# One attention layer of an encoder trunk: TensorE's order in the attention stage written by streams with an account of time, weighing on ScalarE, modulations' totals behind their sums

## The chip, the cores and the metric

The kernel runs on one core of one Trainium2 chip. The core has five engines that run side by side: TensorE (PE, matrix products; PEld is its loading of weights), VectorE (DVE), ScalarE (ACT), GpSimd (POOL) and SyncE (SP), which here issues the DMAs. Each engine works off its own queue in order, and waits at an instruction whose inputs or whose place for the output are not ready. The metric is the time of one execution in microseconds (us).

## What is computed

A trunk of two layers over 256 tokens of 1024 channels: an RWKV-7 layer and an attention layer, each followed by a mixture of experts with 32 experts of 256 hidden channels. The change lies in the attention layer, whose mixer is this:

```python
def dilated_attention_mix(h, w_qkv, w_o):
    qkv = jnp.einsum('bsd,de->bse', h, w_qkv)
    qkv = qkv.reshape(bsz, s, N_GROUPS, 3, ATTN_HEADS, ATTN_HEAD_DIM)      # 3 groups, 8 heads of 128
    for gi, (window, dil) in enumerate(((128, 1), (512, 4), (2048, 16))):
        o, lse = _dilated_group(q, k, v, slopes[gi], window, dil)            # softmax over a window, with ALiBi
    alpha = jax.nn.softmax(jnp.stack(lses), axis=0)                          # groups merged per head
    merged = jnp.sum(alpha[..., None] * o, axis=0).reshape(bsz, s, d)
    return jnp.einsum('bsd,de->bse', merged, w_o)
```

Every sub-layer is normalised, and modulated by six vectors that are products of `silu(c)` with matrices of 1024 x 1024:

```python
    mod = silu_c @ ada_w[i] + ada_b[i]
    sh_t, sc_t, ga_t, sh_c, sc_c, ga_c = jnp.split(mod, 6, axis=-1)
    x = x + ga_t * tm
```

Four of the attention layer's six, numbers m = 2 (`ga_t`), 3, 4 and 5, are computed during its attention, since nothing needs them earlier: `ga_t` is needed by the output weights, 3 and 4 by the router of the experts behind, 5 by those experts.

## The kernel before

The program is four stages in a row: RWKV, its experts (moe 0), attention, its experts (moe 1). The text below is on the attention stage, which in the trace runs from about 675 to 951 us.

**Products in halves.** All attention products are made of two fp16 halves of each operand: `triple` (L1712) issues three matmuls, high x high and the two mixed ones. So every tensor has to be split: `split` (L461) writes the high half on ScalarE (`wh`, `qh`, `eh`, `mh`) and the low half on VectorE (`wl`, `ql`, `el`, `ml`), or, for one half of some weights, on GpSimd.

**Projections.** `project(hp, g)` makes for a pair of heads hp (of four) and a group g (of three) the queries, keys and values, j = 0, 1, 2: 36 projections b = 9 hp + 3 g + j. Each takes one weight tile of 1 MB (`wring`), which is split in two halves; the split halves have three places (`WB`). Each is 48 matmuls of 256 columns into one PSUM bank; there are three such banks (`pp`), and a bank is free again when its projection has been split into `qh`, `ql`. The four output products of the stage's end use the same three banks and one more.

**Scores and merge.** `scores` makes the scores of a (hp, g), 12 matmuls, adds the ALiBi bias (`E`, VectorE, L1800), takes the row maximum (`st`) and the exponential with its sums (ScalarE, L1809). When all three groups of a pair are there, `merge` computes the groups' weights (`mm`, `wg`, `den`: a chain of small VectorE instructions, with one on ScalarE in it). `values(hp, a)`, for each head a of the pair, multiplies the exponentials by these weights, twelve instructions per pair on VectorE (L1837), transposes them on TensorE (`eT`), splits them (`eh`, `el`), multiplies by the values (`av`, 18 matmuls) and splits the result (`mh`, `ml`). The output product (`wo`) uses `mh`, `ml` and the output weights, which GpSimd first multiplies by the gate `ga_t` (`gated`, L583).

**Modulations.** A modulation is 8 tiles of 512 KB (`aring`). `ada` (L428) adds each, times `silu`, to an accumulator `acc` on VectorE, in two half sums of 512 columns (L374 for the first tile, L376 for the others: 64 in the stage). With the eighth tile the total over the partitions is made at once by TensorE (`ada` in the trace: 2 matmuls of 512 columns, or 8 of one column), and VectorE adds the bias. There is one accumulator, so the next modulation's first sum waits until the total has been read.

**What sets the order.** A scheduler places the instructions on the engines; it works with priorities from the order in which the program is written, and with costs of its own. In this stage nothing is pinned: the loop over hp and g below writes projections, then scores of the group before, then four modulation tiles (`ADA_PARTS`); merge and values come at the end of a pair. In the RWKV stage another way is used: `weave` runs several generators (streams), keeps an account of TensorE's time from estimates per matmul, and at each step continues the stream of best rank (`RANK`) that is due. A generator yields either a number, the time in us after which it wants to go on, or a condition. During `weave` TensorE's instructions keep the order in which they are written (`on_pe`); for the other engines the account sets priorities, moved by `OFFSET`.

**DMA.** SyncE issues all weight loads, each waiting until its buffer is free. The weight stream runs through all stages, so the first tiles of moe 1 are loaded while the last projections run; further buffers are added as areas of the attention stage come free (`middle`, `ext`).

Of the kernel before, what the change touches and what calls it, by code (L numbers as in the profile page):

```python
# [10 lines left out]
F32 = mybir.dt.float32  # L11
I32 = mybir.dt.int32
F16 = mybir.dt.float16
# [6 lines left out]
D = 1024  # L20
# [214 lines left out]
def trunk(ctx, tc, names, aps, out, stages=("rwkv", "moe0", "attn", "moe1"), dbg=None, ring=2):  # L235
# [192 lines left out]
    def ada(i, m, k, tag="ps"):  # L428
# [9 lines left out]
        if k < KD - 1:  # L438
            return
        if m in (2, 5):  # L440
            g = gates[i, m] = const.tile([128, D], F32, name=f"ga{m}", tag=f"ga{m}", bufs=1)
            bias = nc.scalar.dma_start(out=g, in_=ap["p_adab"][i:i + 1, m * D:(m + 1) * D].to_broadcast([128, D]))
            tc.keep_in_program_order(bias)
            for c in range(2):
                s = slice(c * 512, c * 512 + 512)
                ps = bank(name="ada", tag=tag)
                mm(ps, ONES, acc[:, s])
                V.tensor_tensor(out=g[:, s], in0=g[:, s], in1=ps, op=ALU.add)
        else:
# [1272 lines left out]
    def heads(outer, mh, ml, before, c4):  # L1722
# [45 lines left out]
        def project(hp, g):  # L1768
            out = []
            for j in range(3):  # L1770
                with tc.issue_after(heads.hi[5].ins) if hp + g == 0 and j == 1 else nullcontext():
                    w = heads.w if hp + g + j == 0 else weights(
                        outer, stream.take(("qkv", hp, g, j)).rearrange("p (k n) -> p k n", k=KD),
                        pool_half=j != 1 and hp + g > 0)
                ps = bank(name="qkv", tag="pp")
                t = [(held, pool)[j // 2].tile([128, 2, S], F16, name=f"q{n}{g}{j}", bufs=1) for n in "hl"]
                for k in range(KD):
                    hk = (hh[:, k], hl[:, k])
                    lhs, rhs = (w[k], hk) if j < 2 else (hk, w[k])
# [4 lines left out]
                split(*(v.rearrange("p a n -> p (a n)") for v in t), ps, (scale if j == 0 else 1.0) / WSC)  # L1784
                out.append(t)
            return out

        def scores(hp, g, qkv, E, st):

            q, k, _ = qkv  # L1790
            w = KW[g]
            for a in range(2):
# [10 lines left out]
                V.tensor_reduce(out=st[:, :, a, 0], in_=e, axis=AX.X, op=ALU.max)  # L1803
            neg = pool.tile([128, NTT, 2], F32, name="neg", bufs=2)
# [26 lines left out]
        def values(hp, a, qkv, E, wg):  # L1831

            eh, el = (pool.tile([128, 8, 128], F16, name=n) for n in ("eh", "el"))
            for g in range(3):
                for t in range(NTT):
                    e = E[g][:, a, t * KW[g]:(t + 1) * KW[g]]
                    V.tensor_scalar(out=e, in0=e, scalar1=wg[:, t, g, a:a + 1], scalar2=None, op0=ALU.mult)  # L1837
            blocks = [E[0][:, a, t * 256 + kt * 128:t * 256 + kt * 128 + 128] for kt in range(2) for t in range(NTT)]
            blocks += [E[g][:, a, t * 128:(t + 1) * 128] for g in (1, 2) for t in range(NTT)]
            for n in range(2):  # L1840
# [3 lines left out]
                split(*(v[:, 4 * n:4 * n + 4].rearrange("p b n -> p (b n)") for v in (eh, el)), ps, WSC)  # L1844
            po = bank(name="av", tag="eT")
            vcol = slice(a * 128, a * 128 + 128)

            def av(o, v, c, start, stop):
                triple(o, [t[:, v[1], vcol] for t in qkv[v[0]][2]],
# [4 lines left out]
            for g in (1, 2):  # L1854
                for t in range(NTT):
# [3 lines left out]
                  po[:, 0:S].rearrange("p (r l) -> p r l", r=NTT), 1.0 / WSC)  # L1859

# [4 lines left out]
        attn_shares = iter(ADA_ATTN)  # L1865
        for hp in range(4):
            if hp == 3:
                modulations_attn[0].done()
                apool1.release()
                if "moe1" in stages:  # L1870
                    ext.extend(middle(1, 0))
            qkv, E, st = [], [], []
            for g in range(4):
                if g < 3:
                    qkv.append(project(hp, g))
                for n in range(max(0, g - 1), g):
                    E.append(pool.tile([128, 2, NTT * KW[n]], F32, name=f"E{n}", bufs=1))
                    st.append(pool.tile([128, NTT, 2, 2], F32, name=f"st{n}", bufs=2))
                    scores(hp, n, qkv[n], E[n], st[n])
                if g < 3 and hp < 3:  # L1880
                    for a in itertools.islice(attn_shares, ADA_PARTS[3 * hp + g]):
                        ada(*a, "ada")
            if hp == 3:
                held.release()
                if "moe1" in stages:
                    ext.extend(middle(1, 4))
            wg = merge(st)
            for a in range(2):
                values(hp, a, qkv, E, wg)
            if hp == 3:  # L1890
                po = {(t, c): bank(name="wo", tag="ada" if t + c == 2 else "pp")
                      for t in range(NTT) for c in range(2)}
                for _ in out_pairs(outer, range(3), po, mh, ml):
                    pass
# [204 lines left out]
```

## Time and profile before

| | us |
|---|---|
| three runs | 1184.41, 1186.47, 1190.94 (median 1186.47) |
| the profiled execution | 1182.29, of which its span 1180.5 |
| attention stage in the span | about 675 to 951 |
| experts behind it (moe 1) | about 964 to 1180 |

| engine | busy us of the span | share |
|---|---|---|
| PE | 1040.8 | 88% |
| DVE | 616.8 | 52% |
| ACT | 432.4 | 37% |
| POOL | 148.7 | 13% |

The span is the time from the first to the last instruction; the 1.8 us by which the execution is longer lie around it. Busy shares are averages over stages with different limits, so each stage has to be read for itself. Matmuls are pipelined, and their shown durations overlap: a projection's matmul is shown with some 273 ns, and the next starts 109 ns later. Where a line is that of a helper (L271 is every matmul), the group is told by its tiles' names.

### The profile page before, as it was taken

Reading aid. Unit: us, or ns where it says so; the run is one execution under the profiler, and the core shown is the slowest. Engines: PE = TensorE matmul, PEld = TensorE weight load, DVE = VectorE, ACT = ScalarE, POOL = GpSimd, SP = SyncE. Lnnn points to the kernel's source line nnn. Section 1 sums busy time; section 2 is a strip of 40 time slices with the busy share of each in tenths; the row PEclk is TensorE's granted clock in tenths of the full one; section 3 lists DMA queues with packets and bytes.
Section 4 is the critical chain, followed back from the end, with each engine's and each line's share of the span. In section 5 each row is a group of like instructions: output and inputs, shape, how many; then the busy total and the mean of one; then the engine's idle time right before and its main releaser. Section 6 shows DMA issues by size and latency. Waiting matters only on the chain.

```text
span 1180.5 us, 25023 instructions
## 1 busy us (share of the span) xinstructions
PE 1040.8 (88%) x10580; PEld 682.5 (58%) x10580; DVE 616.8 (52%) x1458; ACT 432.4 (37%) x915; POOL 148.7 (13%) x110
## 2 busy tenths in 40 slices
PE   7789999998978998978987799899979999789886
PEld 2576677766757655435442388777858754354422
DVE  4864678578485446213111467988885762131112
ACT  2634455455445342101000377555544621010012
POOL 1100010010012600000000112123373000000000
PEclk9879899899988899989999999998989999899999
DMA  9561524325233676998999987877744589989995
GB/s 366 207 220 60 180 67 159 114 89 167 73 130 132 263 286 250 400 414 361 422 421 421 420 346 262 310 268 284 255 173 150 212 352 395 416 362 421 420 421 238
DMA packets 53197, 322.01 MB, mean 273 GB/s; under 512 B 5922, under 2 KB 6562, under 8 KB 21458
## 3 DMA queue, kind: packets, MB, share of 16 engines
q1 hardware_dynamic: 51986, 315.88, 68.7%
q0 software_dynamic: 800, 3.36, 0.8%
q8 instruction: 87, 1.43, 0.5%
q10 hardware_dynamic: 288, 1.05, 0.3%
q14 instruction: 36, 0.29, 0.1%
HBM read 319.22 MB, written 1.05 MB: 271 GB/s over the span
## 4 chain that ended last, share of the span: by engine, by line
PE 23%; DMA 21%; DVE 8%; ACT 2%; issue 1%; ACTq 0%; SPq 0%; DVEq 0%
DMA wring<-in_w_moe_dram 21%; PE qkv L271 11%; PE gu L271 3%; DVE acc L376 2%; PE xT L271 1%; PE wo L271 1%; DVE wl L473 1%; PE acc L271 1%; PE dn L271 1%; PE av L271 1%; PE eT L275 1%; PE sc L271 1%; ACT sq L491 0%; DVE ql L473 0%; DVE E L1837 0%
## 5 line engine op out<-in xcount | busy, mean ns | idle before, releaser
L271 PE MATMUL gu<-wring,xT 128*32 128x512 f32 x1024 | 132.5, 617 | 18.0 <-DMA wring<-in_w_moe_dram 10.8
L376 DVE SCALAR_TENSOR_TENSOR acc<-aring,silu,acc 128x512 f32<-128x512 f32 x140 | 116.1, 859 | 13.2 <-DMA aring<-in_w_ada_dram 13.0
L467 POOL TENSOR_TENSOR wl<-wring,wh 128x1024 f16<-128x1024 f32 x24 | 57.7, 2406 | 409.4 <-DMA wring<-in_w_qkv_dram 248.3
L271 PE MATMUL qkv<-hl,wh 128*128 128x256 f16 x384 | 106.2, 277 | 2.0 <-DVE hl L1762 2.0
L271 PE MATMUL qkv<-hh,wh 128*128 128x256 f16 x384 | 106.3, 277 | 1.6 <-ACT hh L1761 1.6
L271 PE MATMUL qkv<-hh,wl 128*128 128x256 f16 x384 | 106.1, 277 | 1.2 <-DVE wl L473 1.1
L271 PEld LDWEIGHTS gu<-wring,xT 128*32 128x32 f32 x1024 | 31.3, 112 | 101.5 <-issue 78.1
L271 PEld LDWEIGHTS <-wh 128*128 128x128 f16 x768 | 76.3, 100 | 13.1 <-issue 3.6
L271 PE MATMUL dn<-wring,hidT 128*32 128x256 f32 x1024 | 66.2, 407 | 18.1 <-ACT hidT L1564 18.1
L473 DVE SCALAR_TENSOR_TENSOR wl<-wring,wh 128x1024 f16<-128x1024 f32 x56 | 70.6, 1266 | 16.6 <-ACT wh L469 16.6
L271 PE MATMUL acc<-y,back 128*128 128x512 f32 (+1 forms) x144 | 64.2, 568 | 10.3 <-DVE y L1591 8.1
L469 ACT ACTIVATE wh<-wring 128x1024 f16<-128x1024 f32 x56 | 58.6, 1050 | 35.6 <-PE qkv L271 30.9
L271 PEld LDWEIGHTS xT<-oh,x 128*128 128x128 f32 x512 | 59.0, 192 | 21.1 <-issue 9.2
L1366 DVE SCALAR_TENSOR_TENSOR sg<-sg,gu 128x256 f32<-128x256 f32 x16 | 6.7, 420 | 119.3 <-ACT sg L1365 119.3
L271 PE MATMUL xT<-oh,x 128*128 128x128 f32 x512 | 63.5, 280 | 2.5 <-DVE oh L1475 2.5
L1591 DVE TENSOR_TENSOR y<-dn,ga 128x512 f32<-128x512 f32 x28 | 19.4, 692 | 87.1 <-PE dn L271 55.5
L1365 ACT ACTIVATE sg<-gu 128x256 f32<-128x256 f32 x16 | 6.1, 384 | 147.3 <-PE gu L271 147.3
L271 PEld LDWEIGHTS dn<-wring,hidT 128*32 128x32 f32 x1024 | 32.3, 116 | 48.0 <-ACT hidT L1564 22.0
L271 PE MATMUL qkv<-wl,hh 128*128 128x256 f16 x192 | 54.0, 281 | 0.0
L271 PE MATMUL qkv<-wh,hh 128*128 128x256 f16 x192 | 53.9, 281 | 0.0
L271 PE MATMUL qkv<-wh,hl 128*128 128x256 f16 x192 | 53.9, 281 | 0.0
L1507 ACT ACTIVATE back<-bT 128x256 f32<-128x256 f32 x16 | 6.2, 386 | 129.7 <-PE acc L271 129.7
(355 smaller groups left out, 2096.5 us busy)
## 6 DMA issues: line engine op xcount, KB each, us to landing
wring<-in_w_moe_dram SPq DMA_DIRECT2D x192, 1024.0 KB, 19.8
aring<-in_w_ada_dram SPq DMA_DIRECT2D x96, 512.0 KB, 4.7
wring<-in_w_qkv_dram SPq DMA_DIRECT2D x36, 1024.0 KB, 8.7
wring<-in_w_kr_dram SPq DMA_DIRECT2D x8, 1024.0 KB, 5.4
wring<-in_w_vl_dram SPq DMA_DIRECT2D x8, 640.0 KB, 4.6
wring<-in_w_rwo_dram SPq DMA_DIRECT2D x4, 1024.0 KB, 8.2
wring<-in_w_ato_dram SPq DMA_DIRECT2D x4, 1024.0 KB, 6.9
x<-in_x_dram POOLq DMA_DIRECT2D x2, 512.0 KB, 7.7
```

Of the source, the lines that this page charges most:

```text
L271: return on_pe(nc.tensor.matmul(out=o, lhsT=lhsT, rhs=rhs, start=start, stop=stop, **kw))
L275: return on_pe(nc.tensor.transpose(o, i, IDENT[0:i.shape[0], 0:i.shape[0]]))
L376: V.scalar_tensor_tensor(out=acc[:, s], in0=w[:, s], scalar=silu[:, k:k + 1], in1=acc[:, s], op0=ALU.mult, op1=ALU.add)
L467: eng.tensor_tensor(out=lo, in0=src, in1=hi, op=ALU.subtract)
L469: A.activation(out=hi, in_=src, func=AF.Copy, scale=by)
L473: V.scalar_tensor_tensor(out=lo, in0=src, scalar=by, in1=hi, op0=ALU.mult, op1=ALU.subtract)
L1365: A.activation(out=o, in_=ps[:, 0:256], func=AF.Tanh, scale=0.5)
L1366: V.scalar_tensor_tensor(out=o, in0=o, scalar=1.0, in1=ps[:, 0:256], op0=ALU.add, op1=ALU.mult)
L1507: A.activation(out=back, in_=ps[:, 0:S], func=AF.Copy)
L1591: V.tensor_tensor(out=y, in0=py[c], in1=gates[i, 5][:, c * 512:(c + 1) * 512], op=ALU.mult)
```

## The change

The loop over hp and g is replaced by eight streams under `weave`, so that TensorE's order in the whole stage is fixed by the account:

- K, `all_weights`: takes each weight tile and splits its halves as soon as a place of the three is free; best rank. The output weights of the first three units are taken and gated here too.
- P, `splits`: the split of each projection. T, `all_scores`: 2.6 us after the key's split. U, `all_values`: merge, then the weighing, then after 11 us (8 for the last pair) the transposes and products, with 1.0 and 3.2 us between them.
- N, `attn_modulations`: one tile every 4.2 us from the fourth projection on; `attn_totals`: the total 14 us behind its eighth tile. The accumulator has two places.
- Q, `projections`, and O, `output`, fill TensorE otherwise.

The weighing of the exponentials goes from VectorE (`tensor_scalar`) to ScalarE (`activation` with Copy and a scale), for both heads at once, ahead of the transposes. Nothing else is computed in another way. The core of the diff:

```diff
-RANK = dict(X=0, C=1, R=2, F=3, D=4, G=5, S=6, H=6, W=7, A=2.5)
-OFFSET = dict(X=0, C=-6, R=-4, F=-2, D=-2, G=-1, S=0, H=0, W=0, A=8)
-
-ADA_PARTS, PACE = (4, 4, 4, 4, 4, 4, 4, 4, 0), 4.0
+RANK = dict(X=0, C=1, R=2, F=3, D=4, G=5, S=6, H=6, W=7, A=2.5, K=-1, P=-1, T=0, U=1, N=2, Q=8, O=9)
+OFFSET = dict(X=0, C=-6, R=-4, F=-2, D=-2, G=-1, S=0, H=0, W=0, A=8, K=-6, P=-4, T=-3, U=-3, N=2, Q=0, O=0)
+
+PACE, ATTN_PACE, ATTN_LAG = 4.0, 4.2, 14.0
...
-            ada_acc.append(mods.pools[0][0].tile([128, D], F32, name="acc", tag="acc", bufs=1))
+            ada_acc.append(mods.pools[0][0].tile([128, D], F32, name="acc", tag="acc", bufs=1 + (mods is not modulations)))
...
+        def all_weights():
+
+            for b in range(2):
+                halves[b] = heads.w[4 * b:4 * b + 4]
+                done.add(("w", b))
+            for b in range(1, 36):
+                hp, g, j = b // 9, b // 3 % 3, b % 3
+                for k in range(2):
+                    yield after(("half", 2 * b + k - WB))
...
+                        halves[2 * b + k] = half(w, KD, k, P if k and j != 1 and b >= 3 else None)
...
+        def projections():
+            for b in range(36):
...
+                if b == 28:
+                    yield after(("modulations", 0))
+                    modulations_attn[0].done()
+                    apool1.release()
...
+                yield after(("split", b - 3))
...
+                    if k % 4 == 0:
+                        yield after(("w", 2 * b + k // 4))
...
+        def splits():
+
+            for b in range(36):
+                hp, g, j = b // 9, b // 3 % 3, b % 3
+                yield after(("project", b), ("values", hp - 1) if j == 2 else ("scores", 3 * (hp - 1) + g))
...
+        def all_scores():
+            for hp in range(4):
+                for g in range(3):
+                    yield after(("split", 9 * hp + 3 * g + 1), ("values", hp - 1))
+                    yield 2.6
...
+        def all_values():
+            for hp in range(4):
+                yield after(("scores", 3 * hp + 2))
+                wg = merge([sts[hp, g] for g in range(3)])
+                E = [Es[hp, g] for g in range(3)]
+                for a in range(2):
+                    weigh(a, E, wg)
+                yield 11.0 if hp < 3 else 8.0
+                yield after(*(("split", 9 * hp + 3 * g + 2) for g in range(3)))
+                for a in range(2):
+                    yield from values(hp, a, [qkvs[9 * hp + 3 * g + 2] for g in range(3)], E)
+                done.add(("values", hp))
+
+        def attn_modulations():
+            yield after(("project", 3))
+            for i, m, k in ADA_ATTN:
+                ada(i, m, k, "ada", False)
+                if k == KD - 1:
+                    done.add(("sum", m))
+                yield ATTN_PACE
+
+        def attn_totals():
+            for m in (2, 3, 4, 5):
+                yield after(("sum", m))
+                acc = ada_acc[-1]
+                if m in (2, 5):
+                    bias = gate_bias(1, m)
+                yield ATTN_LAG
+                yield from ada_total(1, m, acc, "ada", bias)
+                ada_settle()
+            done.add(("modulations", 0))
+
+        def output(po):
+            yield after(("project", 35), ("split", 35))
+            for t in range(NTT):
+                for c in range(2):
+                    po[t, c] = bank(name="wo", tag="ada" if t + c == 2 else "pp")
...
-                    V.tensor_scalar(out=e, in0=e, scalar1=wg[:, t, g, a:a + 1], scalar2=None, op0=ALU.mult)
+                    A.activation(out=e, in_=e, func=AF.Copy, scale=wg[:, t, g, a:a + 1])
...
+        weave((all_weights(), "K"), (splits(), "P"), (all_scores(), "T"), (all_values(), "U"),
+              (attn_modulations(), "N"), (attn_totals(), "N"), (projections(), "Q"), (output(po), "O"))
```

What stands in the queues, at three places. First VectorE at the first pair's values, before (`wg` is the groups' weights, `E_...` the exponentials of one group, `acc` a modulation's sum):

```order
L1828 TENSOR_TENSOR wg<-wg,den 128x2x2 x3
L1837 TENSOR_SCALAR E_9184<-E_9184,wg 128x256 x2
L1837 TENSOR_SCALAR E_9425<-E_9425,wg 128x128 x2
L1837 TENSOR_SCALAR E_9468<-E_9468,wg 128x128 x2
L1837 TENSOR_SCALAR E_9184<-E_9184,wg 128x256 x2
L473 SCALAR_TENSOR_TENSOR el<-eT,eh 128x512 x2
L376 SCALAR_TENSOR_TENSOR acc<-aring,silu,acc 128x512 x4
L473 SCALAR_TENSOR_TENSOR ml<-av,mh 128x2x128
```

and now:

```order
L376 SCALAR_TENSOR_TENSOR acc<-aring,silu,acc 128x512 x2
L483 SCALAR_TENSOR_TENSOR ql_9583<-qkv,qh_9582 128x512
L483 SCALAR_TENSOR_TENSOR el<-eT,eh 128x512
L376 SCALAR_TENSOR_TENSOR acc<-aring,silu,acc 128x512 x4
L483 SCALAR_TENSOR_TENSOR el<-eT,eh 128x512
L483 SCALAR_TENSOR_TENSOR wl<-wring,wh 128x1024
L483 SCALAR_TENSOR_TENSOR ql_9667<-qkv,qh_9666 128x512
L483 SCALAR_TENSOR_TENSOR ml<-av,mh 128x2x128
L376 SCALAR_TENSOR_TENSOR acc<-aring,silu,acc 128x512 x2
L456 TENSOR_TENSOR ga_9529<-ga_9529,ada 128x512
```

The weighing is gone from VectorE, four half sums stand between the two `el`, and the first total's last two half sums stand behind the `ml` of the first `av`.

Second, TensorE at the same modulation's total (`ada`), before, inside a projection:

```order
L271 LDWEIGHTS wh
L271 MATMUL qkv<-hh,wh 128x256
L271 MATMUL ada<-acc,cst 128x512
L271 LDWEIGHTS wl
L271 MATMUL qkv<-hh,wl 128x256
```

and now:

```order
L271 MATMUL av<-eh,ql_9509 128x128
L271 LDWEIGHTS qh_9508
L271 MATMUL av<-el,qh_9508 128x128
L271 MATMUL ada<-acc,cst 128x512
L271 LDWEIGHTS hh
L271 MATMUL qkv<-wh,hh 128x256
```

The total has moved right behind the last matmul of the first head's values.

Third, VectorE at the fourth pair's merge, the end of the stage, before (`ql_11770` is the last projection's split, that of the third group's values):

```order
L1800 SCALAR_TENSOR_TENSOR E_11821<-acst,sc 128x256 x2
L1803 TENSOR_REDUCE st_11822<-E_11821 128x2
L473 SCALAR_TENSOR_TENSOR ql_11770<-qkv,qh_11769 128x512
L1803 TENSOR_REDUCE st_11822<-E_11821 128x2
L1800 SCALAR_TENSOR_TENSOR E_11847<-acst,sc 128x256
L1805 TENSOR_SCALAR neg<-st_11822 128x4
L1800 SCALAR_TENSOR_TENSOR E_11847<-acst,sc 128x256
L1803 TENSOR_REDUCE st_11848<-E_11847 128x2 x2
L1815 TENSOR_TENSOR mm<-st_11605,st_11822 128x4
```

and now (the same split is `ql_11924`):

```order
L1940 TENSOR_TENSOR wg<-st_11834,mm 128x2x2
L1943 TENSOR_TENSOR den<-wg,st_11490 128x4
L1945 TENSOR_TENSOR mm<-wg,st_11614 128x4
L1946 TENSOR_TENSOR den<-den,mm 128x4
L1945 TENSOR_TENSOR mm<-wg,st_11834 128x4
L1946 TENSOR_TENSOR den<-den,mm 128x4
L1947 RECIPROCAL den<-den 128x4
L1949 TENSOR_TENSOR wg<-wg,den 128x2x2
L483 SCALAR_TENSOR_TENSOR wl<-wring,wh 128x1024
L1949 TENSOR_TENSOR wg<-wg,den 128x2x2 x2
L483 SCALAR_TENSOR_TENSOR ql_11924<-qkv,qh_11923 128x512
```

The last projection's split has moved from ahead of the merge to behind it, and behind a weight's split.

## Rows read from the trace of the kernel before

**Rows 1.** The chain of work that ended last, shares of the span by engine.
```profile
PE 23%; DMA 21%; DVE 8%; ACT 2%; issue 1%; ACTq 0%; SPq 0%; DVEq 0%
```
**Rows 2.** Windows: length; PE, PEld, DVE, ACT, POOL busy (instructions); clock; DMA.
```profile
678.10:726.70 48.60, 48.60 (x421) 42.37 (x421) 35.18 (x48) 33.70 (x47) 9.08 (x4) 0.95 0.77 302
726.70:849.40 122.70, 112.61 (x975) 95.63 (x973) 109.50 (x190) 69.05 (x116) 27.80 (x11) 0.94 0.79 292
849.40:951.30 101.90, 93.36 (x798) 75.05 (x795) 68.67 (x129) 52.71 (x103) 40.38 (x23) 0.97 0.53 190
```
**Rows 3.** PE's waits, middle and last stretch: total us, times, longest.
```profile
PE ada L271 <- DVE acc L376: 4.4, 3, 2.6
PE eT L275 <- DVE E L1837: 3.4, 3, 1.7
...
PE eT L275 <- DVE E L1837: 7.8, 1, 7.8
```
**Rows 4.** Windows again, around two of the stretches at half clock.
```profile
813.00:819.80 6.80, 6.80 (x35) 5.49 (x35) 4.37 (x20) 2.49 (x3) 0.00 (x0) 0.50 0.99 395
877.80:884.60 6.80, 3.01 (x14) 2.59 (x15) 5.90 (x17) 1.17 (x2) 2.23 (x2) 0.50 0.33 135
```
**Rows 5.** Middle stretch, DVE's busy time on L376 alone, then L1837.
```profile
726.70:849.40 122.70, 43.59 (x48) 0.94 0.79 292
...
726.70:849.40 122.70, 7.43 (x24) 0.94 0.79 292
```
**Rows 6.** DVE's waits in the middle stretch: total us, times, longest.
```profile
DVE E L1800 <- PE sc L271: 4.1, 3, 2.0
DVE acc L374 <- PE ada L271: 3.2, 2, 1.8
```
**Rows 7.** DVE's timeline: start, us, line, operation, out<-in, shapes, count.
```profile
751.96 0.44 DVE L473 SCALAR_TENSOR_TENSOR ml<-av,mh 128x256 f16<-128x256 f32 x1
...
761.82 1.41 DVE L376 SCALAR_TENSOR_TENSOR acc<-aring,silu,acc 128x512 f32<-128x512 f32 x2
...
773.88 3.27 DVE L376 SCALAR_TENSOR_TENSOR acc<-aring,silu,acc 128x512 f32<-128x512 f32 x2
```
**Rows 8.** ACT's groups in the stage: count, busy us, mean ns, idle before.
```profile
L1809 ACT ACTIVATE E<-E,neg 128x128 f32<-128x128 f32 x32 | 12.4, 390 | 11.0 <-DVE neg L1805 11.0
...
L1809 ACT ACTIVATE E<-E,neg 128x256 f32<-128x256 f32 x16 | 7.9, 497 | 0.9 <-DVE neg L1805 0.9
```
**Rows 9.** The chain in order of time: start, us, what, count.
```profile
713.44 15.62 PE qkv L271 x143
```
**Rows 10.** The chain where a projection ends and is split.
```profile
863.93 0.89 PE qkv L271 x8
...
866.46 0.69 DVE ql L473
```
**Rows 11.** POOL's timeline: a weight's split, and the output weights' gating.
```profile
773.79 2.15 POOL L467 TENSOR_TENSOR wl<-wring,wh 128x1024 f16<-128x1024 f32 x1 [2.77 <-ACT wh L466]
...
868.14 11.89 POOL L590 TENSOR_TENSOR wring<-wring,ga 128x512 f32<-128x512 f32 x8
```
**Rows 12.** The chain at the third pair's merge.
```profile
876.46 1.14 DVE den L1822
...
881.59 0.47 PE eT L275
```
**Rows 13.** The chain at the fourth pair's merge.
```profile
930.10 0.79 PE sc L271 x12
...
936.27 0.16 DVE den L1822
...
937.35 0.31 DVE wg L1828 x3
```
**Rows 14.** The chain near the end, the last of five such pieces.
```profile
1137.12 19.80 DMA wring<-in_w_moe_dram
```

More of the change, by code (lines that the diff above doesn't have):

```diff
@@ L1766, in heads, with after @@
         scale = 128 ** -0.5
[L1768 to L1774, printed above, removed]
+        halves, done, qkvs, Es, sts = {}, set(), {}, {}, {}
+        def after(*what):
+            return lambda: all(w in done for w in what if w[1] >= 0)
@@ new lines, in half @@
+        def half(w, nk, k, eng=None):
+            h, l = (outer.tile([128, nk // 2, 2048 // nk], F16, name=n, tag=n, bufs=WB) for n in ("wh", "wl"))
+            split(h, l, w[:, k * nk // 2:(k + 1) * nk // 2], WSC, eng)
+            return [(h[:, n], l[:, n]) for n in range(nk // 2)]
+        def all_weights():
[6 more added lines that the diff above has]
+                    yield after(("half", 2 * b + k - WB))
+                    if k == 0:
+                        w = stream.take(("qkv", hp, g, j)).rearrange("p (k n) -> p k n", k=KD)
+                    with tc.issue_after(heads.hi[5].ins) if b == 1 and k == 0 else nullcontext():
+                        halves[2 * b + k] = half(w, KD, k, P if k and j != 1 and b >= 3 else None)
+                    done.add(("w", 2 * b + k))
+            for u in range(3):
+                for k in range(2):
+                    n = 72 + 2 * u + k
+                    yield after(("half", n - WB), ("modulations", 0))
+                    if k == 0:
+                        w = gated(stream.take(("ato", u)), gates[1, 2], 2).rearrange("p (k n) -> p k n", k=2)
+                    halves[n] = half(w, 2, k)
+                    done.add(("w", n))
@@ L1783, in project @@
                                k == 0 and a == 0, k == KD - 1)
-                split(*(v.rearrange("p a n -> p (a n)") for v in t), ps, (scale if j == 0 else 1.0) / WSC)
-                out.append(t)
-            return out
+                    if k % 4 == 3:
+                        done.add(("half", 2 * b + k // 4))
+                    yield
+                qkvs[b] = ps
+                done.add(("project", b))
+            yield after(("scores", 11))
+            held.release()
+            if "moe1" in stages:
+                ext.extend(middle(1, 4))
@@ new lines, in all_scores @@
+        def all_scores():
[3 more added lines that the diff above has]
+                    yield 2.6
+                    E = Es[hp, g] = pool.tile([128, 2, NTT * KW[g]], F32, name=f"E{g}", bufs=1)
+                    st = sts[hp, g] = pool.tile([128, NTT, 2, 2], F32, name=f"st{g}", bufs=2)
+                    yield from scores(hp, g, [qkvs[9 * hp + 3 * g + j] for j in range(2)], E, st)
+                    done.add(("scores", 3 * hp + g))
@@ L1829, in merge, with weigh @@
             return wg
[L1831 to L1833 removed]
+        def weigh(a, E, wg):
             for g in range(3):
@@ L1864, in heads @@
             ext.extend(middle(1, 3))
[L1865 to L1894, printed above, removed]
+        po = {}
+        weave((all_weights(), "K"), (splits(), "P"), (all_scores(), "T"), (all_values(), "U"),
+              (attn_modulations(), "N"), (attn_totals(), "N"), (projections(), "Q"), (output(po), "O"))
         pool.release()
```

46 lines of the change are left out of this document (36 added, 10 removed).

## The prediction

> **What bounds the kernel now.** I read the chain of waits first, then the attention stage in windows, then who waits for whom there, then single places. The chain [rows 1] is TensorE and DMA: the DMA share belongs to the two expert stages, TensorE's share to the attention stage and what lies between. The attention stage runs from 678.10 to 951.30, and its three stretches differ [rows 2]. In the first, to 726.70, TensorE is busy all 48.60 us. In the middle, to 849.40, TensorE is busy 112.61 of 122.70 us and VectorE 109.50: both nearly full, VectorE on the work that TensorE waits for. In the last TensorE is busy 93.36 of 101.90, VectorE 68.67.
>
> TensorE's named waits in the middle are the modulations' totals for their sums, 4.4 us, and the transposes for the weighed scores, 3.4; in the last stretch one wait of 7.8 for the same weighing [rows 3]. Each cluster of such waits is followed by a stretch at half the granted clock (0.50, which is 1.2 of 2.4 GHz): 6.8 us after the waits at 807 to 813, 6.8 around the long one [rows 4], and two more of 3.4 us each at 755.0 and 778.8. At half clock half of the busy time is lost. So TensorE's own work in the middle is 112.61 - (3.4 + 3.4 + 6.8) / 2 = 105.8, and in the last stretch 93.36 - 3.01 / 2 = 91.9. What a perfect order could win is 16.9 + 10.0 = 26.9 us.
>
> **The middle stretch.** TensorE's matmuls only change places there. What counts is VectorE's load, and it falls little. The 24 weighings (7.43 us) go to ScalarE. Against that, the order now begins the sums later: 4 half sums stand ahead of the split of projection 7, where 10 stood, so 60 instead of 54 fall into this stretch; 6 more at 43.59 / 48 = 0.91 us each [rows 5] add 5.4. VectorE's work becomes 109.50 - 7.43 + 5.4 = 107.5, more than TensorE's 105.8. Its idle time was 122.70 - 109.50 = 13.2. Of that 3.2 was the next modulation's first sum waiting until a total had read the only accumulator, and 4.1 the bias step waiting for scores [rows 6]. The second accumulator ends the one; the scores, which now stand half a projection behind their key split with sums on VectorE between, end most of the other. I keep the remaining 5.9: 107.5 + 5.9 = 113.4, a gain of 9.3. Bounds: TensorE alone, 105.8 (gain 16.9), and all of VectorE's idle time kept, 120.7 (gain 2.0).
>
> The 7.6 us that TensorE then still stands have places in the new order. VectorE has the first total's last two half sums behind the split of the first `av`, and TensorE has that total right behind this `av`: a copy, a split (0.44) and a half sum, about 0.45 + 0.44 + 0.7 = 1.6. The second `el` of that head pair stands behind four half sums, 4 x 0.7 = 2.8 [rows 7]. The other three totals have their sums done in good time.
>
> The weighing on ScalarE is not in the trace of before. The nearest rows are its exponentials of the same tiles, 390 ns and 497 ns [rows 8]: at most 32 x 0.390 + 16 x 0.497 = 20.4 us over the stage, half of it in the middle. ScalarE is busy 69.05 of 122.70 there [rows 2], so as load it is free; what it may cost is the delay of the `eh` copies behind twelve of them in a row, and that is in the 5.9 and its bounds.
>
> **The first stretch.** Its three groups of scores stand 24 matmuls behind the key split's projection, 24 x 15.62 / 143 = 2.6 us of cover [rows 9], where 48 stood. With a weight split's ScalarE half ahead, as the new order has it, the chain from a projection's end to the finished split took from 864.82 to 867.15, 2.3 us [rows 10]; with its VectorE half ahead too it is about 1.1 longer. I take 0.5 for the stretch, bounds 0 and 3.
>
> **The last stretch.** Two waits matter. The third head pair's merge runs while GpSimd gates the output weights, one unbroken 11.89 us from 868.14 [rows 11]. A `den` that takes 0.16 us undisturbed [rows 13] took 1.14 there, and the transposes began at 881.59 [rows 12]. GpSimd's order is unchanged and hangs on the same buffers, so it meets the merge again. TensorE now has 84 projection matmuls and one total over it, about 10 us; I put the weighed scores at 13 us behind the scores, a wait of 3 (0 to 8), and 1.5 of half clock. The second wait is new: the last value split. It stood ahead of the fourth pair's merge on VectorE; now it stands behind `den`, `wg` and a weight split. In before the scores ended at 930.89, `den` came 5.4 us behind and `wg` ended at 937.66 [rows 13]; a weight split and the value split add 1.1 and 0.7, so it would be ready 8.6 us behind the scores; less about 0.7 for the second group's exponentials, which are now done earlier, 7.9. The third output bank is that projection's bank, and TensorE is there after 24 + 6 matmuls, 2.6 + 1.3 = 3.9. I take a wait of 4.0 (0 to 6) and 1.5 of half clock. Small waits for scores add 1.5. Together 11.5 against the 10.0 of before: a loss of 1.5, bounds a gain of 8 and a loss of 7.
>
> **Behind the stage.** The second expert stage ends on DMA, five pieces of nearly 20 us back to back, the last at 1137.12 [rows 14]. Its loads start as the attention stage's buffers come free, so I pass a gain on one to one; the least I can defend is 0.8.
>
> **The sum.** -9.3 + 0.5 + 1.5 = -7.3 us. The profiled execution took 1182.29 (span 1180.5), which gives 1175.0. It lies 4.2 below the median of the three runs, 1186.47; against that the same change gives 1179.2. I predict 1179.
>
> **Rivals.**
> *TensorE at its own pace.* If VectorE's queue keeps ahead and both late waits are hidden, the stage shrinks by 16.9 + 8 = 25: 1161.5. For it: TensorE's waits are all for VectorE, and the new order spreads its work. Against: 107.5 us of VectorE work do not fit into 105.8.
>
> *Sums in more places are held more often.* In the middle VectorE had 48 of the half sums of the accumulating form in 43.59 us. Two take 1.41 when GpSimd is still and 3.27 when it splits a weight beside them, 1.9 more [rows 7, 11]. So (43.59 - 48 x 0.7) / 1.9 = 5.3 hits, in 21 runs of sums between other work; in the new order there are 34 runs. At the same odds that is 3.3 hits more, 6.2 us of VectorE time, which leaves a gain of 1: 1185. Against it: a longer run is open to a hit for longer. The Trainium skill says on its page "SBUF — State Buffer", section "Who interferes with whom", that a VectorE instruction with two SBUF inputs contends with a GpSimd instruction that reads SBUF, and that the loser is blocked for the whole instruction; on the pair that took 3.27 this trace agrees. By that rule alone, a run that starts at random would be hit as often as GpSimd is busy (27.80 of 122.70, 23%): 5 hits in 21 runs and 8 in 34, an estimate that gives the same 1185 or so.
>
> *Slower.* TensorE's order is a list made by an account, and 12 groups of scores and 8 of values now stand where the account says that their inputs are ready. If VectorE is behind at these 20 places by one held sum, 1.9 each, TensorE stands 38 us against the 26.9 that it could win: 11 us slower, 1197.5. It decides from a mean wait of 1.35 us per place. Against it: in the first and last stretch VectorE has much idle time [rows 2].
>
> *That it does not do what it says* I leave out: the order of the new kernel shows the moves.
>
> **Chances.** Forecast (a gain of 3 to 14) 0.45; TensorE at its own pace 0.15; sums held more often 0.26; slower 0.14. A measurement of this kernel can tell some 0.5%, 5.9 us, from no change. Of the forecast 0.38 lies beyond that, so faster 0.38 + 0.15 = 0.53; same 0.07 + 0.22 = 0.29; slower 0.14 + 0.04 = 0.18. The range 1163 to 1192 takes in the forecast's bounds, the third case, half of the second and the milder part of the fourth; some 0.16 is left out.
>
> **What would show it.** VectorE busy over 93% from projection 7's split to projection 23's, and that stretch at 110 to 117 us; totals waiting once for a sum, by 1.5 to 3, and no first sum waiting for a total; no VectorE weighing; a TensorE wait of some 4 us in front of the third output bank, with VectorE's last `ql` behind `wg`; a wait of transposes in the third pair while GpSimd gates. It is wrong if VectorE has slack in the middle while TensorE stands, if TensorE's waits there stay under 3 us in all, or if the second expert stage takes back over a third of the gain.

## The result: slower by 0.8%

| kernel | median us | ratio to the kernel before, same chip | 95% interval |
|---|---|---|---|
| before, beside the changed kernel | 1185.10 | | |
| changed | 1195.81 | 1.0082 | 1.0060 to 1.0105 |

The forecast was 1179, a gain of 7; the change costs some 10 us. The ratio leaves out one run of the kernel before, which took 1338.03 us, and is not exactly the quotient of the medians. The profiled executions differ by more, spans of 1180.5 and 1196.1; that of the changed kernel is the slowest of its twelve. Their 15.6 us are used below to find the place, the ratios for the size.

The three stretches of [rows 2] in the changed kernel (length; PE, PEld, DVE, ACT, POOL busy; clock; DMA share and GB/s):

```profile
679.20:731.30 52.10, 49.96 (x432) 43.23 (x432) 33.23 (x48) 36.01 (x56) 8.53 (x4) 0.94 0.84 333
731.30:863.80 132.50, 113.67 (x985) 97.77 (x985) 107.62 (x175) 77.23 (x148) 25.81 (x12) 0.92 0.70 251
863.80:967.50 103.70, 94.46 (x778) 74.36 (x776) 65.00 (x96) 56.74 (x111) 37.62 (x23) 0.95 0.56 200
```

The stage begins 1.1 us later, the first stretch is 3.5 longer, the middle one 9.8, the last 1.8. That is all; from the first output sum on both kernels take 224 us. VectorE's load in the middle came out as computed (107.62 for a forecast of 107.5), but it is spread over 132.50 us and not over 113: VectorE stands idle 24.9 us there, 13.2 before. So the forecast's picture of a full VectorE is wrong at the root. The chain that ended last [rows 1] shows it too; TensorE's share fell, and DMA's with it:

```profile
PE 17%; DMA 13%; DVE 7%; ACT 3%; issue 2%; ACTq 0%; DVEq 0%; SPq 0%
```

TensorE's waits over the stage, then VectorE's in the middle stretch (total us, times, longest; compare [rows 3, 6]):

```profile
PE sc L271 <- DVE ql L483: 7.9, 9, 1.8
PE sc L271 <- ACT qh L479: 5.9, 2, 4.2
PE eT L275 <- ACT E L1956: 5.8, 3, 3.3
PE av L271 <- DVE el L483: 4.4, 3, 3.2
PE wo L271 <- DVE ql L483: 3.6, 1, 3.6
PE ada L271 <- DVE acc L376: 2.1, 1, 2.1
```
```profile
DVE acc L376 <- DMA aring<-in_w_ada_dram: 9.7, 8, 2.2
DVE wl L483 <- ACT wh L479: 5.2, 4, 1.9
DVE el L483 <- ACT eh L479: 2.8, 2, 2.1
DVE ql L483 <- ACT qh L479: 2.0, 1, 2.0
```

New are the scores' waits for the q and k splits (13.8 us; in the kernel before TensorE waited for none by that name) and VectorE's for modulation tiles (9.7; 0.9 before). Both meet at the longest of the scores' waits. VectorE's timeline ahead of it (start, us, what; in brackets the idle time before it and what ended it):

```profile
776.51 0.75 DVE L376 SCALAR_TENSOR_TENSOR acc<-aring,silu,acc 128x512 f32<-128x512 f32 x1
777.17 1.22 DVE L483 SCALAR_TENSOR_TENSOR wl<-wring,wh 128x1024 f16<-128x1024 f32 x1
778.31 2.62 DVE L376 SCALAR_TENSOR_TENSOR acc<-aring,silu,acc 128x512 f32<-128x512 f32 x1
780.85 0.68 DVE L483 SCALAR_TENSOR_TENSOR ql<-qkv,qh 128x512 f16<-128x512 f32 x1
781.45 0.15 DVE L1926 TENSOR_SCALAR neg<-st 128x4 f32<-128x4 f32 x1
781.52 1.40 DVE L376 SCALAR_TENSOR_TENSOR acc<-aring,silu,acc 128x512 f32<-128x512 f32 x2
784.84 0.75 DVE L376 SCALAR_TENSOR_TENSOR acc<-aring,silu,acc 128x512 f32<-128x512 f32 x1 [1.92 <-DMA aring<-in_w_ada_dram]
785.50 1.22 DVE L483 SCALAR_TENSOR_TENSOR wl<-wring,wh 128x1024 f16<-128x1024 f32 x1
786.64 0.68 DVE L483 SCALAR_TENSOR_TENSOR ql<-qkv,qh 128x512 f16<-128x512 f32 x1
```

TensorE is there from 780.74 on, and waits twice, 4.18 us for the `qh` and 1.81 for the `ql`. Two things stand in the way of `ql` at 786.64: a sum that waits for its tile, and a weight split. ScalarE has the same order, a weight's `wh` ahead of the `qh`, but ahead of both it had stood 3.90 us for `neg`:

```profile
781.64 0.51 ACT L1930 ACTIVATE E<-E,neg 128x256 f32<-128x256 f32 x1 [3.90 <-DVE neg L1926]
...
783.62 1.04 ACT L479 ACTIVATE wh<-wring 128x1024 f16<-128x1024 f32 x1
784.57 0.57 ACT L479 ACTIVATE qh<-qkv 128x512 f16<-128x512 f32 x1
```
```profile
785.19 0.27 PE L271 MATMUL sc<-qh,qh 128*128 128x128 f16 x1 [4.18 <-ACT qh L479]
785.25 0.31 PE L271 MATMUL sc<-qh,ql 128*128 128x128 f16 x1
787.38 0.26 PE L271 MATMUL sc<-ql,qh 128*128 128x128 f16 x1 [1.81 <-DVE ql L483]
```

VectorE made `neg` at 781.45, though the maxima that it reads were done at 776.60: ahead of it stood two half sums, one of them of 2.62 us, a weight split and a q split. So most of the 4.18 us at this place comes from what stands ahead of `neg`; the `wh` adds its 1.04.

Nor was TensorE at full clock behind it (window: PE busy 4.00 of 6.80, granted clock 0.50, so 1.2 of 2.4 GHz):

```profile
784.20:791.00 6.80, 4.00 (x25) 3.04 (x25) 6.13 (x11) 3.12 (x5) 2.55 (x1) 0.50 0.60 225
```

A waiting sum holds up what stands behind it. ScalarE wrote a weight's high half by 769.79, and VectorE was idle from 770.01 on, but the low half, which does not need the tile, ran only behind the sum:

```profile
768.73 1.06 ACT L479 ACTIVATE wh<-wring 128x1024 f16<-128x1024 f32 x1 [0.74 <-PE qkv L271]
```
```profile
771.66 0.75 DVE L376 SCALAR_TENSOR_TENSOR acc<-aring,silu,acc 128x512 f32<-128x512 f32 x1 [1.66 <-DMA aring<-in_w_ada_dram]
772.33 1.22 DVE L483 SCALAR_TENSOR_TENSOR wl<-wring,wh 128x1024 f16<-128x1024 f32 x1
```

The Trainium skill says on its page "PSUM — Partial Sum Buffer", section "Engine vs sequencer instructions", that the queues of ScalarE, VectorE and GpSimd are strictly first in, first out. The row at 772.33 agrees.

So there were two suspects. **W**: the rule "weights split first" (streams K and P) puts a weight split, and its wait for `wh`, ahead of nearly every q split. Between a projection's end and its `ql` a `wl` was started in all 36 cases, in 9 before; from that end to the finished `ql` it took 4.7 us on average, 2.8 before. Each of the nine `ql` for which scores waited has a `wl` directly ahead. **L**: modulation tiles that land late. Beside them there were three others: **D**, scores too soon behind their splits in the account, **S**, the sums on VectorE in whatever order, and **A**, ScalarE's weighings.

### The profile page after: what moved, and what is told of

Same layout as the page of the kernel before. It is cut to its first block, busy times and chain, and to the rows that moved or that the text cites. A ratio compares the mean times of both kernels' runs of the same rounds, so it can differ in the third digit from the quotient of the medians.

```text
span 1196.1 us, 25090 instructions
## 1 busy us (share of the span) xinstructions
PE 1043.0 (87%) x10580; PEld 683.8 (57%) x10580; DVE 608.9 (51%) x1410; ACT 446.4 (37%) x963; POOL 143.6 (12%) x110
## 5 line engine op out<-in xcount | busy, mean ns | idle before, releaser
L376 DVE SCALAR_TENSOR_TENSOR acc<-aring,silu,acc 128x512 f32<-128x512 f32 x140 | 113.0, 830 | 23.8 <-DMA aring<-in_w_ada_dram 23.5
L477 POOL TENSOR_TENSOR wl<-wring,wh 128x1024 f16<-128x1024 f32 x24 | 52.1, 2175 | 426.4 <-ACT wh L476 400.0
L271 PE MATMUL dn<-wring,hidT 128*32 128x256 f32 x1024 | 66.3, 407 | 18.0 <-ACT hidT L1574 18.0
```

The lines of the kernel that those rows point to most:

```text
L271: return on_pe(nc.tensor.matmul(out=o, lhsT=lhsT, rhs=rhs, start=start, stop=stop, **kw))
L376: V.scalar_tensor_tensor(out=acc[:, s], in0=w[:, s], scalar=silu[:, k:k + 1], in1=acc[:, s], op0=ALU.mult, op1=ALU.add)
L477: eng.tensor_tensor(out=lo, in0=src, in1=hi, op=ALU.subtract)
```

## The experiments

All are edits of the changed kernel unless said otherwise. Ratios are to the kernel before on the same chip (its medians there 1182.4 to 1184.0); the changed kernel's is 1.0082. e1 and e2 leave out 31 of the 32 loads of modulation tiles, e7 and e8 also seven of eight sums.

| run | median us | ratio | 95% interval |
|---|---|---|---|
| e1 one modulation tile | 1187.36 | 1.0029 | 1.0001 to 1.0056 |
| e2 the same, kernel before | 1190.65 | 1.0059 | 1.0035 to 1.0083 |
| e3 tiles on GpSimd's queue | 1199.85 | 1.0152 | 1.0111 to 1.0193 |
| e4 weighing on VectorE | 1198.55 | 1.0120 | 1.0074 to 1.0166 |
| e5 q splits first | 1181.48 | 0.9979 | 0.9956 to 1.0002 |
| e6 scores later | 1193.72 | 1.0083 | 1.0049 to 1.0116 |
| e7 no sums | 1176.72 | 0.9931 | 0.9900 to 0.9963 |
| e8 no sums, kernel before | 1172.40 | 0.9892 | 0.9859 to 0.9925 |
| e9 weights first, doubled | 1190.97 | 1.0064 | 1.0032 to 1.0095 |
| e10 half tiles | 1189.05 | 1.0046 | 1.0015 to 1.0077 |
| e11 = e5, weighing on VectorE | 1185.89 | 1.0020 | 0.9998 to 1.0042 |
| e12 = e5, totals later | 1183.85 | 1.0011 | 0.9989 to 1.0034 |
| e13 = e5 and e10 | 1175.89 | 0.9936 | 0.9911 to 0.9961 |
| e14 = e13, gate's second half later | 1175.06 | 0.9931 | 0.9905 to 0.9957 |
| e15 half tiles, kernel before | 1185.42 | 1.0025 | 1.0003 to 1.0047 |

### First round: loads or weighing

e1 and e2, in the changed kernel and in the one before:

```diff
...
-        modulations_attn.append(Stream(nc.sync, pool, [(a, ap["w_ada"][a]) for a in ADA_ATTN], 2, D, "aring"))
+        held_tile = pool.tile([128, D], F32, name="aring", tag="aring")
+        nc.sync.dma_start(out=held_tile, in_=ap["w_ada"][ADA_ATTN[0]])
+        modulations_attn.append(SimpleNamespace(pools=[[pool]], take=lambda a: held_tile, done=lambda: None))
```

> The changed kernel, but the attention stage's 64 half sums all read one modulation tile that is loaded once, at the stage's start; it leaves out the other 31 loads of 512 KB (so the modulations' values are not those wanted). Sums, totals, weights and TensorE's order stay. Theory L (the loss comes from loads: a sum stands in VectorE's queue before its tile has landed, because its load stands in SyncE's queue behind a weight load that waits for a split, and everything behind the sum waits too): the stage loses its excess, 1180 us or less, VectorE's waits for the modulation tile (10.5 us in the changed kernel) at 0, TensorE's waits for scores under 5 us of 13.8. Rival D (TensorE's fixed order has scores too soon behind VectorE's split, whatever the loads do): within 4 us of the changed kernel's 1195.8, waits for scores stay above 10. Rival A (ScalarE's twelve weighings in a row): also within 4 us.

> The kernel before with the same omission: its sums in the attention stage all read one modulation tile that is loaded once (31 loads of 512 KB left out). It is the control for the traffic itself. Theory L: the kernel before loses little to these loads (VectorE waits 2.3 us for them there), so it gains under 5 us, to 1180 to 1185. If fewer bytes alone help, it gains as much as the changed kernel does from the same omission.

e3 replaces `nc.sync` by `nc.gpsimd` in that Stream:

> The changed kernel with the attention stage's modulation loads issued from GpSimd's queue and no longer from SyncE's, where they alternate with weight loads. Theory L: a modulation load now waits only for its own buffer, so VectorE's wait for the tiles falls from 10.5 us to under 4 and the time to 1183 to 1190; part may be lost since GpSimd's weight splits now stand behind such a wait. Rivals D and A: 1193 to 1198, or slower through GpSimd's splits.

e1 fell short of L's 1180, and e2 got slower with 16 MB less to load. In e1 VectorE's wait for tiles is gone, but the scores' waits are 15.0 us in its trace, where L expected under 5. Both runs changed more than meant: a tile that is always there lets the scheduler put sums earlier. In e1 22 half sums stand ahead of projection 7's `ql`, where the changed kernel has 4; in e2 24, where the kernel before has 10. They fill the first stretch:

```profile
677.70:737.00 59.30, 52.56 (x432) 44.52 (x432) 47.53 (x68) 38.74 (x58) 11.72 (x5) 0.90 0.72 285
737.00:858.10 121.10, 111.65 (x996) 97.26 (x996) 89.17 (x158) 75.25 (x145) 23.08 (x11) 0.96 0.43 146
```

In e1 that stretch is 7.2 us longer than in the changed kernel, the middle 11.4 shorter (its profiled run is the slowest of its ten). e3 did the same (26 half sums ahead, a first stretch of 66.3, a middle of 123.2, and slower in all); its tiles came later and not sooner: VectorE waited 27.7 us for them, where L expected under 4. These three don't decide on L. That sums ahead of splits cost TensorE time wherever they stand fits all three, but each changed the loads as well.

```diff
-                    A.activation(out=e, in_=e, func=AF.Copy, scale=wg[:, t, g, a:a + 1])
+                    V.tensor_scalar(out=e, in0=e, scalar1=wg[:, t, g, a:a + 1], scalar2=None, op0=ALU.mult)
```

> The changed kernel with one part undone: the 48 weighings are on VectorE again, as before. Rival A (twelve weighings in a row on ScalarE hold back the copies that the transposes, the weight splits and the q splits need): 5 us faster or more, 1191 or less. Theories L and D: VectorE gets some 15 us more work over the stage, in a stretch where it stands idle a fifth of the time but in front of TensorE: 1196 to 1202.

A falls: with the weighing back on VectorE the kernel is no faster, here and in e11.

### Second round: the order of splits, the scores, the sums

```diff
-RANK = dict(... K=-1, P=-1 ...)
-OFFSET = dict(... K=-6, P=-4 ...)
+RANK = dict(... K=0, P=-1 ...)
+OFFSET = dict(... K=-4, P=-6 ...)
```

> The changed kernel with one part undone: of a q split and a weight split that stand to be issued together, the q split comes first again (rank and offset of the two streams exchanged). Theory W (the rule 'weights split first' puts a weight split of 1.15 us, and the wait for its ScalarE half, ahead of the q split on VectorE; 26 of 36 q splits have one directly ahead in the changed kernel, 15 in the kernel before): the lag from a projection's end to its finished split falls by about 0.6 us on average, TensorE's waits for scores from 13.8 us to under 6, the time to 1184 to 1190. Theory S (the half sums of the modulations stand ahead of q splits and scores, whatever order the splits have): 1192 to 1199, since 13 q splits now have a half sum directly ahead in place of a weight split.

This is the main result: 1.0082 becomes 0.9979, some 12 us, in an exchange that leaves TensorE's and GpSimd's order as it is, row for row, and moves only VectorE's and ScalarE's rows and some loads. The same place in the changed kernel and in e5, behind projection 4:

```profile
711.37 1.40 DVE L376 SCALAR_TENSOR_TENSOR acc<-aring,silu,acc 128x512 f32<-128x512 f32 x2
712.70 1.21 DVE L483 SCALAR_TENSOR_TENSOR wl<-wring,wh 128x1024 f16<-128x1024 f32 x1
713.83 0.68 DVE L483 SCALAR_TENSOR_TENSOR ql<-qkv,qh 128x512 f16<-128x512 f32 x1
```
```profile
705.84 1.41 DVE L376 SCALAR_TENSOR_TENSOR acc<-aring,silu,acc 128x512 f32<-128x512 f32 x2
707.57 0.69 DVE L483 SCALAR_TENSOR_TENSOR ql<-qkv,qh 128x512 f16<-128x512 f32 x1 [0.33 <-ACT qh L479]
708.52 1.83 DVE L483 SCALAR_TENSOR_TENSOR wl<-wring,wh 128x1024 f16<-128x1024 f32 x1 [0.25 <-ACT wh L479]
```

In the first TensorE's scores waited 1.74 us for that `ql`, in the second not at all. Over e5's stage the waits for scores are 2.4 us, the lag from a projection's end to its `ql` is 3.6 on average, and a `wl` was started in it in 14 cases; what waits more is the projections, for weights:

```profile
PE qkv L271 <- DVE wl L483: 7.4, 6, 1.6
PE ada L271 <- DVE ga L456: 6.0, 1, 6.0
PE ada L271 <- DVE acc L376: 2.7, 1, 2.7
...
PE sc L271 <- ACT qh L479: 1.4, 1, 1.4
...
PE sc L271 <- DVE ql L483: 1.0, 2, 0.6
```

VectorE's wait for modulation tiles is still 9.0 us in e5, so W is a cause without L.

e6 is `yield 5.2` for `yield 2.6` in `all_scores`:

> The changed kernel with the scores twice as far behind their key split in TensorE's order: 5.2 us of account in place of 2.6, as the kernel before had it with a whole projection. Theory D (the account gives VectorE too little time between a key split and the scores): TensorE's waits for scores fall from 13.8 us to under 5, the time to 1183 to 1190. Theories S and W (VectorE's own order holds the split back by up to 6 us and the rest follows): the waits move to other places, 1192 to 1200.

D's cure fails: the waits for scores go (3.5 us are left), the time stays. With scores later, other steps become late: projections wait 11.0 us for GpSimd's weight halves, a total waits 9.5 for its sum.

e7 and e8, on top of e1 and e2:

```diff
-        ada_add(acc, w, k, k == 0)
+        if k == 0 or mods is modulations:
+            ada_add(acc, w, k, k == 0)
```

> The changed kernel without seven of eight sums of each modulation in the attention stage, and without their loads: only the first sum and the total are left of each (it leaves out 56 of 64 half sums, 50 us of VectorE, and 31 loads). Theory S: TensorE's waits in the stage fall to a third, the stage to TensorE's own pace: 1165 to 1175. Theories W and D: a good part of the waits stays, 1180 or more.

> The kernel before with the same omission (56 of 64 half sums and 31 loads left out). Control for the run above: what the order of the kernel before loses when the sums are no burden. Theory S: it gains 10 us or more and stays slower than the changed kernel without sums by some 5 us, since its totals and weighings still wait as they did. Theories W and D: the kernel before is the faster of the two even so.

Without sums the changed kernel is still not faster than the one before (1176.7 and 1172.4; the intervals just overlap), as W and D said and S did not. Its time lies between S's 1165 to 1175 and the 1180 or more of W and D. By the ratios the sums and their loads cost 0.0151 or 18 us in the new order, 0.0108 or 13 in the old one; that would be right of S, but the intervals don't settle the difference.

### Third round: dose, tiles, what else

e9: `K=-10, P=0`.

> The changed kernel with 'weights first' made stronger: the weight splits' offset from -6 to -10 and the q splits' from -4 to 0, ranks as they are. Theory W (a weight split ahead of a q split on VectorE costs): no better than the changed kernel, 1195 to 1205, TensorE's waits for scores 14 us or more. Rival L' (what the exchange of e5 changed is rather how early the weights' loads are issued): weights that are split even earlier release their buffers earlier, 1190 or less.

No cure, and no more harm either: within the changed kernel's interval, under the 1195 to 1205 that W expected, with 12.9 us of waits for scores for an expected 14 or more. In the changed kernel a `wl` was started in every one of the 36 lags already, so there was little dose to add. L' (e5 works by the time at which weights are loaded) would have it under 1190; the median lies just above that, and neither gain nor loss can be told from the changed kernel. Against L', ScalarE's wait for weight tiles rose, from 19.9 to 27.7 us.

e10 (`ada` takes the tiles in halves, too):

```diff
...
-        pool = tc.alloc_tile_pool(name="apool1", bufs=2, side="right", reuse_waits="tile")
-        modulations_attn.append(Stream(nc.sync, pool, [(a, ap["w_ada"][a]) for a in ADA_ATTN], 2, D, "aring"))
+        pool = tc.alloc_tile_pool(name="apool1", bufs=5, side="right", reuse_waits="tile")
+        modulations_attn.append(Stream(nc.sync, pool, [((a, e), ap["w_ada"][a][:, e * 512:e * 512 + 512]) for a in ADA_ATTN for e in range(2)], 5, 512, "aring"))
```

> The changed kernel with its modulation tiles loaded in halves (512 columns) into five buffers of half size, where it has two of full size: 25% more room and a buffer free after each half sum. Theory L (loads that come late): VectorE's wait for the tiles from 10.5 us to under 5, the time to 1184 to 1190. Theory W: the wait for the tiles falls or not, but the lag from projection to split stays and the time is 1192 to 1199.

VectorE's wait for tiles falls from 10.5 to 1.0 us and the middle stretch to 120.4; the ratio by 0.0036, with intervals that overlap. The waits for scores stay (11.9). By this run alone L is a smaller second cause, if one.

> The splits-first kernel of e5 with the 48 weighings on VectorE again, as the kernel before has them. If VectorE is what the stage hangs on, 15 us more work on it cost 3 to 8 us against e5's 1181.5: 1184 to 1190. If the order of splits is all that matters, 1180 to 1183.

> The splits-first kernel of e5 with the modulations' totals further behind: 18 us of account in place of 14 behind their last sum, and 8 in place of 2.5 between the two halves of a gate's total. In e5's trace TensorE stood 2.8 us in front of the first total and 6.2 in front of the second half of the last one, which waits for a VectorE step behind the third pair's merge; behind these waits it ran at half clock for 3.4 and 6.8 us, 5 us lost. If these waits end and nothing takes their place: 1169 to 1174. If the merge holds other work in their stead: 1178 to 1182.

e11's ratio is 0.0041 above e5's, some 5 us: the move of the weighing to ScalarE is worth about that, as it is from the changed kernel to e4 (0.0038). In e12 the waits for totals went from 8.7 to 0.9 us, as meant, and the time did not fall; its median lies above both of the ranges expected. In the last stretch TensorE now stood 3.3 us in front of weights and 2.6 in front of the transposes, at the same merge.

### Fourth round: both together

> The changed kernel with both: q splits ahead of weight splits (e5, ratio to the kernel before 0.998) and modulation tiles loaded in halves into five half buffers (e10, 1.0046 where the changed kernel has 1.0082). Two causes that add up: 0.998 - 0.0036, so 0.993 to 0.996, 1174 to 1179. One cause: 0.997 to 1.000, no better than e5. In e10's trace the middle stretch took 120.4 us, in e5's 125.1; with both I expect 117 to 121 and VectorE's wait for modulation tiles under 3 us.

> The kernel of e13 with the second half of a gate's total 8 us of account behind the first in place of 2.5 (the last total waited 6.2 us for it in e5's trace; the totals' distance behind their sums stays). If that wait hides nothing: 3 to 8 us faster than e13. If the merge behind it only puts the wait elsewhere, as in e12: within 2 us of e13.

> The kernel before with its modulation tiles in halves and five half buffers. VectorE waits only 2.3 us for these tiles there: if late loads are a matter of the new order alone, ratio 0.998 to 1.001; if the finer loads help any order, 0.995 or less.

e13 beats both kernels, 0.9936. Against e5 that is 0.0043 more (their intervals just overlap), against e10 0.011: the two gains add up, 0.0103 and 0.0036 to 0.0139, measured 0.0146. In the kernel before, the half tiles bring nothing: 1.0025, a little above what was expected, and VectorE's wait for tiles is 6.1 us there, 2.3 without them. So the half tiles are no gain in just any order; that late tiles cost nothing in the old one isn't shown, since e15 took no wait away. e13's windows, VectorE's wait for tiles (under 3 us was expected), and the middle stretch of e5 and of e10:

```profile
676.70:725.20 48.50, 48.33 (x420) 41.90 (x420) 32.80 (x49) 35.38 (x55) 9.86 (x4) 0.94 0.93 369
725.20:845.20 120.00, 110.35 (x1011) 97.33 (x1010) 107.00 (x174) 76.74 (x148) 25.72 (x11) 0.97 0.77 272
845.20:945.20 100.00, 91.33 (x764) 72.67 (x763) 65.83 (x96) 57.12 (x112) 37.55 (x23) 0.97 0.56 207
```
```profile
DVE acc L377 <- DMA aring<-in_w_ada_dram: 3.2, 3, 2.0
```
```profile
724.20:849.30 125.10, 109.40 (x997) 95.29 (x995) 106.83 (x174) 77.24 (x148) 25.32 (x11) 0.99 0.74 262
```
```profile
729.55:849.95 120.40, 107.97 (x996) 95.64 (x996) 107.26 (x174) 77.46 (x148) 26.81 (x12) 0.99 0.78 273
```

e14 adds nothing that can be told from e13: the 6.2 us in front of the gate became 5.0 in front of the transposes, as in e12.

## Why the prediction was wrong, step by step

**The middle stretch, forecast -9.3, measured +9.8: the step that failed.** Its parts were right: 60 half sums lie in it (54 in the accumulating form, 6 first ones), VectorE's load is 107.62, and TensorE's own work, less half of the 15.5 us that it was busy at half clock, is 113.67 - 7.8 = 105.9 for a forecast of 105.8. Wrong is "I keep the remaining 5.9". It struck out VectorE's two largest idle times and took for granted that nothing new would follow; VectorE idled 24.9 us. For TensorE the forecast had 7.6 us of standing here, none of it in front of scores; it stood 18.8 (10.1 before), 9.5 of that in front of scores, and half clock took 1.0 more than before. VectorE idles where the next row of its queue is not ready, and the new order put two such rows ahead of what TensorE needs: weight splits (W, 12 us of the whole time by e5 and the changed kernel) and sums whose tiles are late (L, some 4 to 5 by e10 and by e13 against e5). I had seen the first, "with its VectorE half ahead too it is about 1.1 longer", and charged it to the first stretch alone.

In the middle alone the profiles share the loss out in another way: its 132.5 us become 125.1 in e5, 120.4 in e10 and 120.0 in e13. There the half tiles bring as much by themselves as both changes together, and much of e5's gain lies in the first stretch (3.8) and the last (4.7). These are single executions, the changed kernel's its slowest, so they place the loss and don't weigh the two causes. Even with both changes VectorE idles 13.0 us in e13's middle, as much as before, not 5.9; no run that leaves nothing out comes near the forecast's 113.4 (the least is 119.6, in e14).

**The sums' price.** I took the held ones as the danger. They were held no more than before: 54 take 46.56 us, 0.86 each, for 0.91 [rows 5], and six of them took over 1 us, as six of 48 did before. Counted alike, the runs of such sums between other work are 32, and 20 before. That rival falls.

**The first stretch, forecast +0.5, measured +3.5.** TensorE idles 2.1 us in it, in front of scores, where it was never idle before, and 11 more matmuls lie in it (1.2 us). In e5 it is back to 48.26.

**The last stretch, forecast +1.5, measured +1.8.** Both waits came where they were put: the third output bank 3.6 (4.0), the third pair's transposes 3.3 (3). The first goes to 0.7 in e5, where the last value split runs ahead of `den` again and the weight split behind `wg`; so what stood ahead of it made most of the wait, and the weight split alone 1.2 of it at most.

**Behind the stage.** The loss passed on one to one, as said.

**The marks.** Totals waited once for a sum, 2.1 (1.5 to 3); no first sum waited for a total; VectorE weighs nothing; the last `ql` stands behind `wg`. VectorE was to be busy over 93% of the middle, and is 81%. Against the forecast stood "VectorE has slack in the middle while TensorE stands", and this is what the windows show.

**The slower rival, 1197.5 at 0.14,** had the time and the places, scores and values, but another cause (held sums) and a price that wasn't reached: 7.9 + 5.9 + 4.4 = 18.2 us at its 20 places, 0.9 each, where it asked for 1.35. With the transposes' 5.8 it is 24.0, or 1.2 each; the output bank's 3.6 and the total's 2.1 lie outside its places.

**The weighing's move** was counted as 7.43 us off VectorE in the middle; it is worth some 5 over the whole time (e11 to e5), intervals touching.

What stays open: e5 exchanges the order on VectorE and on ScalarE at once, so how much of its 12 us each carries was not separated. The rows at 712.70 speak for VectorE, those at 783.62 for ScalarE too. e5 also moved some loads. ScalarE's wait for weight tiles in the middle rose from 4.3 us in the kernel before to 19.9, and is 13.7 in e5 and 5.6 in e10 and e13; but it is 18.7 in e8, the fastest kernel of all, so whether it costs time isn't shown.

## What to carry to other kernels

On an engine that works off its queue in order, ask of each row not how long it takes but whether it can stand idle with something urgent behind it: a split that feeds a later product belongs behind the split that the next product waits for, even if it is ready first. An engine's load, however well added up, gives a bound and not a time; the idle time has to be rebuilt for the new order from its waits, and striking out old waits isn't that. An experiment that takes loads away changes a scheduler's order as well, so look at where the instructions went before reading its time.

## What was not expected of the hardware

The modulation tiles were late without a lack of bandwidth: the DMA share in the middle fell from 0.79 to 0.70. The kernel before has the same two buffers and VectorE waited 0.9 us for tiles in its middle, so the buffers alone don't make the wait. With two buffers a load can only start when a sum has ended, and the chain shows the round trip, a load of 4.93 us between two sums:

```profile
765.22 1.41 DVE acc L376 x2
...
766.64 4.93 DMA aring<-in_w_ada_dram
...
771.66 0.75 DVE acc L376
```
